# Row sums of squares by ScalarE from a second layout of x, and layer B's first operands made beside layer A's out-projection

## The chip, the cores and the metric

The kernel runs on one core of a Trainium2 chip. TensorE (PE) does the matrix products, VectorE (DVE) and ScalarE (ACT) prepare their operands and take up their results, GpSimd (POOL) does elementwise sums, and SyncE (SP) issues nearly all DMAs from one in-order queue. The metric is the device time of one execution in microseconds (us); lower is better.

## The reference

Two layers on x of 2048 tokens by 1024 features, all in fp32:

```python
for i in range(2):
    h = rmsnorm(x, norm_g[i])        # x * 1/sqrt(mean(x*x) + eps) * g, per token
    x = x + (recurrent_mixer if i == 0 else shortconv_mixer)(h, ...)
return rmsnorm(x, final_g)
```

Layer A (the recurrent mixer): an in-projection from 1024 to 2 x 1536 channels, a causal convolution of 4 taps, two gates by products of 12 heads of 128, a linear recurrence over the tokens, a SiLU gate, and an out-projection from 1536 to 1024. Layer B (the short convolution): an in-projection from 1024 to 4 x 1536 channels, a convolution of 3 taps between two elementwise products, a SiLU gate and an out-projection.

What matters here is the norm. Each token has one factor 1/sqrt(mean of its squares), and the products need it along the free axis: features lie on the partitions and tokens along the row, so the kernel wants the factor as a tile of 128 x 512 with the same row in each partition.

## The kernel before, in words

**Tiling.** The tokens are cut in four chunks of 512. A chunk of x is eight tiles of 128 features x 512 tokens (xs). A fp32 product is done as three f16 products: each operand is split into a high half (ACT, a copy to f16, L297 for x and L403 for weights) and a low half (DVE, the difference, L299 and L404), and `mm3` multiplies high by high, high by low and low by high (L483, L486, L487) into one of six accumulators in PSUM. A product for layer A or B therefore waits for one DVE instruction per operand tile, the low half. Before the split DVE norms a tile of x in place (L291), which needs the factor `inv`.

**The factors in layer A.** Chunk 0 adds up squares in SBUF and sums them over partitions on PE. Chunks 1, 2 and 3 use `inv_by_products`: ACT squares each of the eight tiles (L269), PE multiplies each by a matrix of ones in fp32 (L272), which sums over the partitions and leaves the result in every partition, ACT takes the root (L276) and DVE the reciprocal of 128 x 512 (L277). The generator `second()` does this for chunks 2 and 3 and makes their operands, while PE runs the first products of layer A (`in_A`).

**The out-projection of layer A** (`outA.run`, its first product at 624.3 us, its last at 876.6 us) goes over 4 chunks x 8 blocks of 128 output features. It calls back `emitA` for each finished block: DVE adds the product to the residual x (L1332), SP stores it as layer B's input x2 (chunks 2 and 3 also stay in SBUF), ACT squares it (L216), POOL adds the squares up (L217). After a chunk `endA` makes its factor: PE sums over partitions (L223), then ACT and DVE make 1/root. For chunks 0 and 2 the result goes through DRAM by two DMAs that POOL issues (L239, L240); for chunk 1 by small fp32 products with a diagonal matrix (dg, pn; L246, L249).

**Beside it** runs `besideA(c, d)` with n = 8c + d, the number of the block. It loads and squares the first two weight units of layer B for their scales (L1355, L365; `unit_scale` sums on PE, L374), makes the weight operands of the first unit (`unit_weights`; the sums of weight blocks ws are POOL's, L455), and makes layer B's first activation operands (`build_h`: B11, T1, T2, B21, B22, T3, T4, for k = 0 to 3; each is an element sum or a plain block of the normed x of chunks 0 and 1, split into halves). Layer B's first unit (`in_B`, `unit`) multiplies A11 by B11 (tile p), S1 by T1 (r), S2 by T2 (q) and so on; p opens at once behind the last block of A.

**Order.** The program is written out by a tile scheduler that sets the order of each engine ahead of time from priorities (`tc.high_priority`) and from the order in the code; `after(a, b)` pins a behind b, `in_order` keeps SP's loads in the order in which they were written. At run time each engine works through its list and stops at the first instruction whose input or buffer isn't ready.

Of the kernel before, what the change touches and what calls it, by code (L numbers as in the profile page):

```python
# [31 lines left out]
FIXED = NPC + P + 1 + 2 * (4 + 2 * KB) + 13 * NH + 2 * NH + 19 + 32 + 3 * CH + 66  # L32
# [14 lines left out]
def trunk(ctx, tc, xT, prm, wa, ga, oa, wb, ob, out):  # L47
# [100 lines left out]
    zjunk = keep(CH)  # L148
    tapt, gut = ([keep(n) for i in range(2)] for n in (8, 1))
# [165 lines left out]
    def build_h(l, x, inv, ks, ops, ready=()):  # L315
# [8 lines left out]

        t1, t2 = {}, {}
        for k in ks:
            norm(k, 0)
            add(ops, "B11", k, x[k, 0])
# [13 lines left out]
        for k in ks:  # L342
            norm(k + 4, 0)
            add(ops, "B21", k, x[k + 4, 0])
# [925 lines left out]
    x1 = {(d, c): load("A", d, 2 + c, xt("xs")) for c in range(2) for d in range(KB)}  # L1270
# [3 lines left out]
    def second():  # L1274
        h = build_blocks(0, x1, inv1, hA[1])
        for c in range(2):
            for _ in range(4 - 2 * c):
                yield
            inv_by_products(
                [x1[d, c] for d in range(KB)], inv1[c], split0[1][0], blocks_last[0]  # L1280
            )
            yield
            for _ in range(2):
                next(h)
                yield
# [43 lines left out]
    early, sws, xB = [], [], {}  # L1329
# [17 lines left out]

    def besideA(c, d):
        n = KB * c + d
        if n in (12, 15):  # L1350
            raw = []
            u = (n - 12) // 3
            for q in range(4):
                raw.append(op32("ws"))
                in_order(sp.dma_start(raw[q], wb[u][:, q * CH : (q + 1) * CH]))  # L1355
            sws.append(unit_scale(1, *unit_squares(raw)))
        if n < 17:
            return
        if n == 17:
            early.append(unit_weights(1, wb[0], w0, sws[0]))  # L1360
        if n in (17, 24):
            ks = (0, 1) if n == 17 else (2, 3)
            x = {
                (k, cc): load("B", k, cc, sgt("xs"))
                for a in ks
                for k in (a, a + 4)
                for cc in range(2)
            }
            early.insert(0, build_h(1, x, inv[0], ks, hB[0]))
        advance(early)  # L1370
        if n >= 24:
            advance(early)
# [13 lines left out]
    for d in range(KB):  # L1386
        normed(1, x[d, 0], d, inv[1][0])
# [203 lines left out]
```

## Time and profile before

| | before |
|---|---|
| median of 3 runs | 2043.05 us (2041.72 to 2635.88) |
| profiled execution | 2048.05 us, span 2046.3 us, mean granted PE clock 0.993 |
| PE busy | 2006.7 us, 98% |
| DVE busy | 1178.1 us, 58% |
| ACT busy | 964.2 us, 47% |
| POOL busy | 522.9 us, 26% |
| DMA | 167.22 MB, mean 82 GB/s |

The span is that of the profiled execution, from the first to the last instruction; its own time is 1.75 us longer. Engine shares are means over very different stretches, so the page's table by slices and the windows of the trace are read beside them. In a row of the trace "x5" stands for five like instructions in a run, and square brackets give the engine's idle time before the row and what ended it. Line numbers are those of the kernel before; in the changed kernel the same lines stand a few further down.

### The profile page before, as it was taken

Reading aid. Unit: us, or ns where it says so; the run is one execution under the profiler, and the core shown is the slowest. Engines: PE = TensorE matmul, PEld = TensorE weight load, DVE = VectorE, ACT = ScalarE, POOL = GpSimd, SP = SyncE. Lnnn points to the kernel's source line nnn. Section 1 sums busy time; section 2 is a strip of 40 time slices with the busy share of each in tenths; the row PEclk is TensorE's granted clock in tenths of the full one; section 3 lists DMA queues with packets and bytes.
Section 4 is the critical chain, followed back from the end, with each engine's and each line's share of the span. In section 5 each row is a group of like instructions: output and inputs, shape, how many; then the busy total and the mean of one; then the engine's idle time right before and its main releaser. Section 6 shows DMA issues by size and latency. Waiting matters only on the chain.

```text
span 2046.3 us, 25185 instructions
## 1 busy us (share of the span) xinstructions
PE 2006.7 (98%) x9366; PEld 949.1 (46%) x9366; DVE 1178.1 (58%) x2042; ACT 964.2 (47%) x1756; POOL 522.9 (26%) x437
## 2 busy tenths in 40 slices
PE   8999999999999999978999999999999999999997
PEld 3444444444444444433444444444444444444476
DVE  8977665657474427579636446437437346463323
ACT  7778786868583423234433342343433423443211
POOL 0011010101010213354543433424424424213220
PEclk9999999999999999989999999999999999999998
DMA  7011213042105523411021021121121110574111
GB/s 239 0 52 57 89 51 104 30 166 91 59 22 180 181 75 146 108 67 42 31 93 33 30 86 38 37 93 42 47 78 37 57 42 6 184 279 145 62 40 49
DMA packets 92859, 167.22 MB, mean 82 GB/s; under 512 B 10368, under 2 KB 14080, under 8 KB 92736
## 3 DMA queue, kind: packets, MB, share of 16 engines
q1 hardware_dynamic: 92176, 164.29, 24.0%
q0 software_dynamic: 560, 1.32, 0.3%
q8 instruction: 73, 1.20, 0.3%
q14 instruction: 50, 0.41, 0.1%
HBM read 123.62 MB, written 41.95 MB: 81 GB/s over the span
## 4 chain that ended last, share of the span: by engine, by line
PE 90%; DVE 5%; issue 2%; DMA 2%; ACT 1%; POOL 1%; SPq 0%; DVEq 0%; POOLq 0%; ACTq 0%
PE acc L486 14%; PE acc L487 14%; PE acc L483 14%; PE q L487 6%; PE q L486 6%; PE q L483 6%; PE pg L839 4%; PE p L487 4%; PE p L486 4%; PE p L483 4%; PE r L483 4%; PE r L486 4%; PE r L487 4%; DVE op L299 2%; DVE xs L291 1%
## 5 line engine op out<-in xcount | busy, mean ns | idle before, releaser
L486 PEld LDWEIGHTS <-wc 128*128 128x128 f16 x2096 | 205.4, 98 | 265.3 <-issue 32.2
L483 PEld LDWEIGHTS <-wc 128*128 128x128 f16 x2096 | 208.2, 99 | 253.1 <-issue 17.6
L487 PEld LDWEIGHTS <-wc 128*128 128x128 f16 x2096 | 205.6, 98 | 257.9 <-issue 16.4
L483 PE MATMUL acc<-zs,wf 128*128 128x512 f16 (+1 forms) x864 | 307.8, 356 | 0.0
L486 PE MATMUL acc<-zs,wf 128*128 128x512 f16 (+1 forms) x864 | 307.7, 356 | 0.0
L487 PE MATMUL acc<-zs,wf 128*128 128x512 f16 (+1 forms) x864 | 306.9, 356 | 0.0
L486 PE MATMUL acc<-op,wc 128*128 128x512 f16 x752 | 284.8, 379 | 2.9 <-DVE op L299 2.9
L487 PE MATMUL acc<-op,wc 128*128 128x512 f16 x752 | 285.0, 379 | 0.0
L483 PE MATMUL acc<-op,wc 128*128 128x512 f16 x752 | 283.8, 379 | 0.0
L483 PE MATMUL q<-op,wc 128*128 128x512 f16 x576 | 218.2, 380 | 7.1 <-DVE pb L522 4.2
L487 PE MATMUL q<-op,wc 128*128 128x512 f16 x576 | 219.5, 381 | 0.0
L486 PE MATMUL q<-op,wc 128*128 128x512 f16 x576 | 219.1, 380 | 0.0
L864 POOL TENSOR_TENSOR u<-fixed,u 128x512 f32<-128x512 f32 x48 | 51.3, 1089 | 564.5 <-ACT fixed L861 564.5
L404 DVE SCALAR_TENSOR_TENSOR wc<-ws,fixed,wc 128x512 f16<-128x512 f32 x100 | 98.3, 985 | 98.2 <-ACT wc L403 97.7
L486 PE MATMUL p<-op,wc 128*128 128x512 f16 x384 | 146.3, 381 | 0.0
L483 PE MATMUL p<-op,wc 128*128 128x512 f16 x384 | 146.3, 381 | 0.0
L487 PE MATMUL p<-op,wc 128*128 128x512 f16 x384 | 146.2, 381 | 0.0
L487 PE MATMUL r<-op,wc 128*128 128x512 f16 x384 | 145.7, 379 | 0.0
L486 PE MATMUL r<-op,wc 128*128 128x512 f16 x384 | 145.5, 379 | 0.0
L483 PE MATMUL r<-op,wc 128*128 128x512 f16 x384 | 145.5, 379 | 0.0
L217 POOL TENSOR_TENSOR sa<-sa,sq 128x512 f32<-128x512 f32 x49 | 66.8, 1363 | 241.8 <-ACT sq L216 224.8
L931 POOL TENSOR_TENSOR pb<-pb,cg 128x512 f32<-128x512 f32 x48 | 65.8, 1371 | 230.0 <-ACT pb L548 149.1
(178 smaller groups left out, 3078.2 us busy)
## 6 DMA issues: line engine op xcount, KB each, us to landing
wr<-in_wb SPq DMA_DIRECT2D x100, 256.0 KB, 3.3
xs<-in_xT SPq DMA_DIRECT2D x48, 256.0 KB, 5.4
zA<-sg SPq DMA_DIRECT2D x48, 256.0 KB, 2.0
zr<-zA SPq DMA_DIRECT2D x48, 256.0 KB, 5.3
zB<-ed SPq DMA_DIRECT2D x48, 256.0 KB, 2.0
zr<-zB SPq DMA_DIRECT2D x48, 256.0 KB, 5.3
wr<-in_wa SPq DMA_DIRECT2D x44, 256.0 KB, 4.0
xr<-x SPq DMA_DIRECT2D x32, 256.0 KB, 5.3
```

Of the source, the lines that this page charges most:

```text
L217: squared[0] = eng.tensor_tensor(out=acc, in0=acc, in1=sq, op=ALU.add)
L291: return v.scalar_tensor_tensor(out=x, in0=x, scalar=gs[l][:, kk : kk + 1], in1=inv, op0=ALU.mult, op1=ALU.mult)
L299: return hi, v.tensor_tensor(out=t[:, 1, :], in0=src, in1=t[:, 0, :], op=ALU.subtract)
L404: v.scalar_tensor_tensor(out=t[:, 1, :], in0=src, scalar=sw[:, 2:3], in1=t[:, 0, :], op0=ALU.mult, op1=ALU.subtract,)
L483: ins = nc.tensor.matmul(acc, wh, xh, start=start, stop=False, **kw)
L486: nc.tensor.matmul(acc, wh, xl, start=False, stop=False, **kw)
L487: return nc.tensor.matmul(acc, wl, xh, start=False, stop=stop, **kw)
L839: ins = nc.tensor.matmul(pg, gw[m][:, oo], u, start=True, stop=True)
L864: g.tensor_tensor(out=u, in0=w, in1=u, op=ALU.mult)
L931: g.tensor_tensor(out=t, in0=t, in1=cg[m, half, c], op=ALU.mult)
```

## The change

**Chunks 2 and 3 of layer A.** `inv_by_products` is no longer called for them. Instead x is also given to the kernel in its token-row layout (`in_xn`, 2048 x 1024; no arithmetic is done outside), four tiles of 128 tokens x 1024 features are loaded per chunk (4 x 512 KB), and ACT squares each in place and sums along the row in the same instruction (`accum_out`). That leaves the sums of 512 tokens as 128 x 4. `inv_from` then makes the factor: a root and a reciprocal of 128 x 4, four diagonal matrices by DVE (dg), four small fp32 products by ones (pn) and a copy of 128 x 512 from PSUM.

**Beside A's out-projection.** The loads and squares for the scales of layer B's first two weight units move from n = 12 and 15 to n = 1 and 3, the first unit's weight operands from n = 17 to n = 5. B11 and B21 (chunk 0) of all k are made at n = 10 to 13, and `build_h`, still started at n = 17 and 24, skips them. The tiles of layer B's x have their own names but lie in the twelve buffers of "xs". From n = 24 on, one step instead of two is taken per block. The norm of chunk 2 moves from behind the out-projection to n = 28 to 31.

```diff
--- before
+++ after
...
@@ -146,6 +146,7 @@
     zsc = [keep(3) for c in range(4)]
     gts = [buf(cst, f"gts{m}", f"gts{m}", 1) for m in range(2)]
     zjunk = keep(CH)
+    rows = [keep(4) for c in range(2)]
     tapt, gut = ([keep(n) for i in range(2)] for n in (8, 1))
     tailt = [[[keep(3) for c in range(4)] for m in range(2)] for i in range(2)]
     ws2 = keep(2 * CH).rearrange("p (m c) -> p m c", m=2)
@@ -322,10 +323,14 @@
                 if evac_last[0] is not None:
                     after(ins, evac_last[0])
 
+        def block(name, k, kk, c):
+            if (name, k) not in ops:
+                norm(kk, c)
+                add(ops, name, k, x[kk, c])
+
         t1, t2 = {}, {}
         for k in ks:
-            norm(k, 0)
-            add(ops, "B11", k, x[k, 0])
+            block("B11", k, k, 0)
         yield
         for k in ks:
             norm(k, 1)
@@ -340,8 +345,7 @@
             add(ops, "T2", k, t2[k])
         yield
         for k in ks:
-            norm(k + 4, 0)
-            add(ops, "B21", k, x[k + 4, 0])
+            block("B21", k, k + 4, 0)
         yield
         for k in ks:
             add(ops, "B22", k, x[k + 4, 1])
@@ -1267,18 +1271,29 @@
     w0["behind"] = split0[1][0]
     run(prep0)
     head = first_done(accs, inv0[0], split0[1][1])
-    x1 = {(d, c): load("A", d, 2 + c, xt("xs")) for c in range(2) for d in range(KB)}
+    x1, xrows = {}, [[], []]
+    for c in range(2):
+        for i in range(4):
+            t = wk.tile([P, D], F32, tag="xn", name="xn", bufs=4)
+            xrows[c].append(t)
+            r0 = (2 + c) * CH + i * P
+            sp.dma_start(t, xn[r0 : r0 + P, :])
+        for d in range(KB):
+            x1[d, c] = load("A", d, 2 + c, xt("xs"))
     run(blocks0)
     constants()
 
     def second():
+
         h = build_blocks(0, x1, inv1, hA[1])
         for c in range(2):
+            for i, t in enumerate(xrows[c]):
+                ins = s.activation(t, t, AF.Square, accum_out=rows[c][:, i : i + 1])
+                after(ins, split0[1][0])
             for _ in range(4 - 2 * c):
                 yield
-            inv_by_products(
-                [x1[d, c] for d in range(KB)], inv1[c], split0[1][0], blocks_last[0]
-            )
+            with tc.high_priority(PR):
+                inv_from(rows[c], inv1[c], None, v.tensor_copy, blocks_last[0])
             yield
             for _ in range(2):
                 next(h)
@@ -1326,7 +1341,7 @@
     run(preA)
 
     hB, inv, sums, w0 = [{}, {}], {}, {}, {}
-    early, sws, xB = [], [], {}
+    early, sws, xB, xh = [], [], {}, {}
 
     def emitA(c, d, xr, acc, undo, ts):
         evac_last[0] = v.scalar_tensor_tensor(
@@ -1345,31 +1360,38 @@
             return
         inv_of(sums[c], inv[c // 2][c % 2], g if c in (0, 2) else None)
 
+    def load_h(kk, c):
+        xh[kk, c] = load("B", kk, c, buf(wk, "xh", "xs", 12))
+
     def besideA(c, d):
+
+
         n = KB * c + d
-        if n in (12, 15):
+        if n in (1, 3):
             raw = []
-            u = (n - 12) // 3
+            u = (n - 1) // 2
             for q in range(4):
                 raw.append(op32("ws"))
                 in_order(sp.dma_start(raw[q], wb[u][:, q * CH : (q + 1) * CH]))
             sws.append(unit_scale(1, *unit_squares(raw)))
-        if n < 17:
-            return
-        if n == 17:
+        if n == 5:
             early.append(unit_weights(1, wb[0], w0, sws[0]))
+        if n >= 10 and n < 14:
+            k = n - 10
+            for kk, name in ((k, "B11"), (k + 4, "B21")):
+                load_h(kk, 0)
+                normed(1, xh[kk, 0], kk, inv[0][0])
+                add(hB[0], name, k, xh[kk, 0])
         if n in (17, 24):
             ks = (0, 1) if n == 17 else (2, 3)
-            x = {
-                (k, cc): load("B", k, cc, sgt("xs"))
-                for a in ks
-                for k in (a, a + 4)
-                for cc in range(2)
-            }
-            early.insert(0, build_h(1, x, inv[0], ks, hB[0]))
+            for k in ks:
+                load_h(k, 1)
+                load_h(k + 4, 1)
+            early.append(build_h(1, xh, inv[0], ks, hB[0]))
+        if n >= 28:
+            for kk in range(2 * n - 56, 2 * n - 54):
+                normed(1, xB[kk, 2], kk, inv[1][0])
         advance(early)
-        if n >= 24:
-            advance(early)
 
     def kept_x(d, c):
         def tile():
@@ -1383,8 +1405,6 @@
     while early:
         run(early.pop(0))
     w0 = w0, ahead(1, wb[1], sws[1])
-    for d in range(KB):
-        normed(1, x[d, 0], d, inv[1][0])
     acc3 = sums[3]
 
     def second_half():
...
```

**How the order of instructions moves.** First, layer A's start, around the factor of chunk 2. On PE, before (ss is the sum of squares, acc the accumulators of A's first units):

```order
L487 LDWEIGHTS wc
L487 MATMUL acc<-op,wc 128x512
L486 LDWEIGHTS wc
L486 MATMUL acc<-op,wc 128x512
L487 LDWEIGHTS wc
L487 MATMUL acc<-op,wc 128x512
L272 MATMUL ss<-sq,fixed 128x512 x8
L483 LDWEIGHTS wc
L483 MATMUL acc<-op,wc 128x512
L486 LDWEIGHTS wc
```

and in the changed kernel (pn is the spread-out factor):

```order
L491 LDWEIGHTS wc
L491 MATMUL acc<-op,wc 128x512
L490 LDWEIGHTS wc
L490 MATMUL acc<-op,wc 128x512
L491 LDWEIGHTS wc
L491 MATMUL acc<-op,wc 128x512
L250 MATMUL pn<-dg,fixed 128x128 x4
L487 LDWEIGHTS wc
L487 MATMUL acc<-op,wc 128x512
```

Eight fp32 products of 512 columns are replaced by four of 128, which wait for DVE's dg instead of ACT's squares. On ACT at the same place, before (sq are the squares of chunk 2, u starts the convolution of the first unit, junk are squares of weights):

```order
L365 ACTIVATE junk,fixed<-w_150 128x512
L365 ACTIVATE junk,fixed<-w_151 128x512
L269 ACTIVATE sq<-xs 128x512
L365 ACTIVATE junk,fixed<-w_152 128x512
L365 ACTIVATE junk,fixed<-w_153 128x512
L269 ACTIVATE sq<-xs 128x512 x5
L800 ACTIVATE u<-xb,fixed 128x512
L269 ACTIVATE sq<-xs 128x512
L800 ACTIVATE u<-xb,fixed 128x512
L269 ACTIVATE sq<-xs 128x512
L297 ACTIVATE op<-xs 128x512
```

and now:

```order
L369 ACTIVATE junk,fixed<-w_150 128x512
L369 ACTIVATE junk,fixed<-w_151 128x512
L1291 ACTIVATE xn,fixed<-xn 128x1024 x4
L369 ACTIVATE junk,fixed<-w_152 128x512
L369 ACTIVATE junk,fixed<-w_153 128x512
L804 ACTIVATE u<-xb,fixed 128x512 x2
L236 ACTIVATE r<-fixed 128x4
L298 ACTIVATE op<-xs 128x512 x2
L1291 ACTIVATE xn,fixed<-xn 128x1024
L896 ACT_TABLE_LOAD
L896 ACTIVATE sg<-acc,fixed 128x512 x2
```

The four long squares of chunk 2 stand ahead of both u; those of chunk 3 follow further back.

Second, DVE in the middle of the out-projection of A, only in the changed kernel (xr is a block's residual, zs the operands of the next chunk of the out-projection, xs and op layer B's x of chunk 0):

```order
L1347 SCALAR_TENSOR_TENSOR xr<-acc,fixed,xr 128x512
L1064 TENSOR_SCALAR fixed<-fixed 128x1
L1072 SCALAR_TENSOR_TENSOR zs<-zr,fixed,zs 128x512 x4
L292 SCALAR_TENSOR_TENSOR xs<-xs,fixed,inv 128x512 x2
L1072 SCALAR_TENSOR_TENSOR zs<-zr,fixed,zs 128x512
L292 SCALAR_TENSOR_TENSOR xs<-xs,fixed,inv 128x512 x4
L1072 SCALAR_TENSOR_TENSOR zs<-zr,fixed,zs 128x512
L300 TENSOR_TENSOR op<-xs,op 128x512
L292 SCALAR_TENSOR_TENSOR xs<-xs,fixed,inv 128x512
L300 TENSOR_TENSOR op<-xs,op 128x512
L292 SCALAR_TENSOR_TENSOR xs<-xs,fixed,inv 128x512
L300 TENSOR_TENSOR op<-xs,op 128x512
```

The eight norms need the factor of chunk 0; half of the zs stand behind the first of them, and so does a block's xr.

Third, the end of A's out-projection. On DVE, before (xs<-acc takes up a block, wc is the low half of a weight, op that of an x operand):

```order
L404 SCALAR_TENSOR_TENSOR wc<-ws,fixed,wc 128x512
L404 SCALAR_TENSOR_TENSOR wc<-wr,fixed,wc 128x512
L404 SCALAR_TENSOR_TENSOR wc<-ws,fixed,wc 128x512
L299 TENSOR_TENSOR op<-t_6719,op 128x512
L299 TENSOR_TENSOR op<-t_6725,op 128x512
L299 TENSOR_TENSOR op<-xs,op 128x512 x4
L404 SCALAR_TENSOR_TENSOR wc<-ws,fixed,wc 128x512
L404 SCALAR_TENSOR_TENSOR wc<-wr,fixed,wc 128x512
L1332 SCALAR_TENSOR_TENSOR xs<-acc,fixed,xs 128x512
L404 SCALAR_TENSOR_TENSOR wc<-wr,fixed,wc 128x512
L1332 SCALAR_TENSOR_TENSOR xs<-acc,fixed,xs 128x512 x3
```

and now:

```order
L1347 SCALAR_TENSOR_TENSOR xs<-acc,fixed,xs 128x512
L344 TENSOR_TENSOR t_6812<-xs,t_6756 128x512
L300 TENSOR_TENSOR op<-t_6806,op 128x512
L300 TENSOR_TENSOR op<-t_6812,op 128x512
L300 TENSOR_TENSOR op<-xs,op 128x512 x4
L300 TENSOR_TENSOR op<-t_6806,op 128x512
L1347 SCALAR_TENSOR_TENSOR xs<-acc,fixed,xs 128x512
L300 TENSOR_TENSOR op<-t_6812,op 128x512
L300 TENSOR_TENSOR op<-xs,op 128x512 x4
L1347 SCALAR_TENSOR_TENSOR xs<-acc,fixed,xs 128x512 x4
```

The weights' low halves among the last blocks are gone, made earlier. On POOL at the same place (sa adds up squares, ws sums weight blocks), before:

```order
L217 TENSOR_TENSOR sa<-sa,sq 128x512
L455 TENSOR_TENSOR ws<-wr 128x512
L217 TENSOR_TENSOR sa<-sa,sq 128x512
L455 TENSOR_TENSOR ws<-wr 128x512
L455 TENSOR_TENSOR ws<-ws,wr 128x512
L217 TENSOR_TENSOR sa<-sa,sq 128x512 x3
L455 TENSOR_TENSOR ws<-wr,ws 128x512
```

and now:

```order
L459 TENSOR_TENSOR ws<-ws,wr 128x512
L218 TENSOR_TENSOR sa<-sa,sq 128x512
L358 TENSOR_TENSOR t_6806<-xs,t_6806 128x512
L358 TENSOR_TENSOR t_6812<-xs,t_6812 128x512
L218 TENSOR_TENSOR sa<-sa,sq 128x512 x5
L459 TENSOR_TENSOR ws<-wr,ws 128x512
L459 TENSOR_TENSOR ws<-wr 128x512
```

The sums of squares of the last five blocks now stand together, with no ws between them.

## Rows read from the trace of the kernel before

**Rows 1.** PE's waits over the span: engine, line, waited for: total us, times, longest.

```profile
PE ss L223 <- POOL sa L217: 7.5, 1, 7.5
...
PE q L483 <- DVE pb L522: 4.2, 1, 4.2
...
PE acc L486 <- DVE op L299: 2.9, 3, 1.7
```

**Rows 2.** Timeline of PE, 20 to 80 us: start us, us, engine, line, op.

```profile
23.75 1.05 PE L249 MATMUL pn<-dg,fixed 128*128 128x128 f32 x8
...
54.46 7.03 PE L272 MATMUL ss<-sq,fixed 128*128 128x512 f32 x16
61.33 0.38 PE L483 MATMUL acc<-op,wc 128*128 128x512 f16 x1
...
71.26 7.03 PE L272 MATMUL ss<-sq,fixed 128*128 128x512 f32 x16
```

**Rows 3.** Timeline of DVE at 63 us and at 894 us.

```profile
63.59 3.35 DVE L277 RECIPROCAL inv<-inv 128x512 f32<-128x512 f32 x1 [2.84 <-ACT inv L276]
...
894.77 0.88 DVE L246 TENSOR_SCALAR dg<-fixed,r 128x128 f32<-128x128 f32 x4
```

**Rows 4.** Timeline of ACT at 39 us, and line L861's long activation (ns min/median/max).

```profile
39.27 2.70 ACT L269 ACTIVATE sq<-xs 128x512 f32<-128x512 f32 x5
...
L861 ACT ACTIVATE fixed<-fixed x24: 1056/1057/1059, 102.4 to 613.4; 128x1024 f32<-128x1024 f32 x24
```

**Rows 5.** Windows: us, then each engine's busy us (instructions), PEclk, DMA share, GB/s.

```profile
23.00:29.00 6.00, 6.00 (x22) 3.13 (x21) 4.09 (x7) 4.66 (x9) 0.00 (x0) 1.00 0.01 2
...
50.00:75.00 25.00, 23.28 (x84) 10.51 (x83) 21.66 (x32) 15.90 (x26) 0.00 (x0) 1.00 0.01 2
```

**Rows 6.** Timeline of PE, 876 to 893 us.

```profile
876.85 0.38 PE L483 MATMUL p<-op,wc 128*128 128x512 f16 x1
877.06 0.38 PE L486 MATMUL p<-op,wc 128*128 128x512 f16 x1
...
882.96 0.38 PE L483 MATMUL q<-op,wc 128*128 128x512 f16 x1 [0.77 <-DVE xs L1332]
...
892.36 1.87 PE L223 MATMUL ss<-fixed,sa 128*128 128x1 f32 x8 [7.52 <-POOL sa L217]
```

**Rows 7.** Windows by stage, the columns of rows 5.

```profile
700.00:725.00 25.00, 25.00 (x117) 11.34 (x116) 10.41 (x17) 13.91 (x29) 5.31 (x5) 1.00 0.53 140
725.00:750.00 25.00, 25.00 (x120) 11.71 (x119) 5.07 (x12) 3.11 (x5) 3.85 (x3) 1.00 0.09 32
...
850.00:875.00 25.00, 25.00 (x118) 11.36 (x116) 25.00 (x24) 13.79 (x25) 18.21 (x12) 1.00 0.13 46
...
895.00:900.00 5.00, 5.00 (x15) 1.83 (x14) 2.06 (x6) 0.14 (x1) 0.00 (x0) 0.56 0.00 0
```

**Rows 8.** Timeline of DVE, 840 to 886 us.

```profile
840.94 6.05 DVE L291 SCALAR_TENSOR_TENSOR xs<-xs,fixed,inv 128x512 f32<-128x512 f32 x9 [3.30 <-DMA inv<-rd]
...
858.18 1.75 DVE L299 TENSOR_TENSOR op<-xs,op 128x512 f16<-128x512 f32 x1
...
872.01 1.28 DVE L299 TENSOR_TENSOR op<-xs,op 128x512 f16<-128x512 f32 x2
...
883.49 2.05 DVE L1332 SCALAR_TENSOR_TENSOR xs<-acc,fixed,xs 128x512 f32<-128x512 f32 x3
```

**Rows 9.** Timeline of POOL, 887 to 893 us.

```profile
887.57 4.73 POOL L217 TENSOR_TENSOR sa<-sa,sq 128x512 f32<-128x512 f32 x3
```

**Rows 10.** Timeline of SP's queue, 645 to 690 us.

```profile
652.07 6.72 SPq L1048 DMA_DIRECT2D zr<-zA  x12
...
679.02 1.64 SPq L1335 DMA_DIRECT2D x<-xr  x2
```

**Rows 11.** Tile ws, 640 to 800 us, its loads' landing; POOL's timeline at 716 us.

```profile
DMA to landing us min/median/max: 5.4/7.7/13.1
...
715.89 0.56 POOL L240 DMA_DIRECT2D inv<-rd  x1 [11.80 <-DMA ws<-in_wb]
```

More of the change, by code (lines that the diff above doesn't have):

```diff
@@ L31 @@
 NPC = 284
-FIXED = NPC + P + 1 + 2 * (4 + 2 * KB) + 13 * NH + 2 * NH + 19 + 32 + 3 * CH + 66
+FIXED = NPC + P + 1 + 2 * (4 + 2 * KB) + 13 * NH + 2 * NH + 19 + 32 + 3 * CH + 66 + 8
 KH = NH // 2
@@ L46, in trunk @@
 @with_exitstack
-def trunk(ctx, tc, xT, prm, wa, ga, oa, wb, ob, out):
+def trunk(ctx, tc, xT, xn, prm, wa, ga, oa, wb, ob, out):
     nc = tc.nc
@@ L1571 @@
         "in_xT": i["x"][0].T,
+        "in_xn": i["x"][0],
         "in_prm": prm,
```

## The prediction

> **What bounds the kernel now.** I read the page's shares first (PE busy 98%, the next engine 58%), then PE's waits, then the timelines where PE stands still or does work that the change removes, and last the engines on which those places wait. PE's whole idle time is some 40 us, and the page's chain of waits gives PE 90% of the span, so a gain can only come from PE work that goes away or from one of the few waits. The largest wait, 7.5 us for POOL's sum of squares, is one that the change bears on; the 4.2 us wait for DVE further on isn't, and the 2.9 us for DVE's low halves lies where the change works [rows 1]. So there are two places: layer A's first 100 us, and the passage from A's out-projection to layer B around 880 us. In between PE is fed without a stop, so what is won at the first place is carried to the second, if nothing new stops PE on the way.
>
> **First place: the squares of chunks 2 and 3.** Removed from PE are two groups of eight fp32 products; each holds PE for 61.33 - 54.46 = 6.87 us, the second like the first [rows 2]: -13.7 us. Added are two groups of four small products, 1.05 us each as the same helper shows for another chunk [rows 2]: +2.1 us. Net -11.6 us of PE work.
>
> Whether PE gets all of it hangs on DVE, which is nearly full here (21.66 of 25 us [rows 5]). Two reciprocals of 3.35 us go, one with 2.84 us of waiting before it [rows 3]. In their place each chunk has four dg at 0.88 us for the four [rows 3] and a copy, which I put at 0.7 us since other 128 x 512 operations on DVE take 0.64 to 0.74 (an estimate from a low half [rows 8]): 1.6 us against 3.35. DVE gains 3.5 us or more, and the waits. But the added dg of both chunks now stand on DVE's queue ahead of low halves of chunk 1, where PE already follows DVE (the 2.9 us [rows 1]). ACT loses sixteen squares at 0.54 us, 8.6 us [rows 4], and gains eight long ones at 1.06 us [rows 4], about 9 us with the read of the sum: even in amount, but four of them, 4.4 us, now stand in a block ahead of the convolution's u, and DVE waits behind that for about 1.6 us (my walk through the new order with these durations: u becomes ready at 43.4 instead of 41.9). While PE follows DVE, to about 62 us, it can't run ahead; by the same walk the product that starts at 61.33 before starts at about the same time after it, with the first 6.87 us spent on waiting for low halves in part. Take 2.6 us for that: gain 9. Ends: 11.6 if DVE never becomes the limit, 6 if both chunks' dg, copies and ACT's block all land on PE's path (11.6 - 2 x 1.6 - 1.6 - 0.8).
>
> The eight loads of the second layout, 4.2 MB, cost nothing in the sum: the first four are issued near 17 us and have the stretch to 29 us, in which the DMA share is 0.01 [rows 5], before ACT wants them at 37.5; the other four wait for the first squares and are wanted from about 46 us. The f32 loads of x behind them on SP's queue come about 8 us later than before but are wanted only from 62 us on.
>
> **The middle: work moved under the out-projection.** All of it is work that was there before, and PE is at work at every moment of this stretch, so it costs nothing as long as nobody's wait reaches PE. The nearest to doing so are three. (1) PE's two sums for the weights' scales wait for ACT's squares, which wait for loads. SP issued its loads of zr from 652.07 and, but for three more loads, was idle before 679.02 [rows 10]; the four loads of the first unit stand behind ten of these, at about 657. Landing took 5.4 to 13.1 us, median 7.7 [rows 11], the four squares some 2.8 us, the same again for the second unit, whose buffers come free with the first squares: 657 + 2 x (7.7 + 2.8) = 678, at the worst 689, against PE reaching the second sum at about 686 (counted back in the new order from 876.85 at 0.2155 us a product, between the 0.21 of [rows 6] and 0.22). I take 0, with 8 as the far end. (2) DVE's norms of chunk 0 wait for the factor that went through DRAM: POOL issued its last DMA at 715.89, held for 11.80 us by weight loads that are now out of its way [rows 11]. It would land by about 727. Behind the norms stand operands of the out-projection's next chunk, which PE wants when that chunk begins, two chunks of 8 x 36 products at 0.2155 us before 876.85, so at 752: 0. (3) The moved norms and low halves, sixteen on DVE at 0.64 to 1.75 us [rows 8], at most 28 us, go where DVE is busy 10.41 and 5.07 of 25 us [rows 7]: 0.
>
> **Second place: the end of the out-projection.** DVE runs without a gap from 840.94 to 885.5 us, through 51 instructions, and the last three blocks of A are taken up at 883.49 only [rows 8], although PE had finished the last block before 876.85 [rows 6]. POOL then sums three squares in 4.73 us [rows 9] with sums of weights queued between, and PE, which comes to its sum of squares at 892.36 - 7.52 = 884.84, waits until 892.36 [rows 6]. After that the clock is granted at 0.56 of full from 895 to 900, which is the lower level of 1.2 GHz for most of it [rows 7].
>
> In the new order the same stretch of DVE's list has 36 instructions; eight low halves of x, and seven of weights, are gone from it. At the stretch's own mean, 44.6 / 51 = 0.87 us, they take 32 us: DVE is at the last block at about 873, ahead of PE. The last block is then taken up at 877.6, squared at 878.3 and added at about 880, while PE reaches its sum at 884.84 - 0.77 = 884.1: 4 us to spare. So 0.77 + 7.52 = 8.3 us of waiting go, and with them the low clock: from 892.36 to about 900, 7.6 us, PE ran at that share and so lost 0.44 x 7.6 = 3.4 us. Together -12. Everything behind starts that much earlier in the same order, and the 4.2 us wait [rows 1] stays.
>
> Here a DVE instruction's time is the unknown. A low half took 1.75 us at 858.18 and 0.64 at 872.01 [rows 8], long ones where POOL was at work. At 0.64 the 36 end at 864, at 1.75 for all at 904, which is later than before; the mean of the stretch is nearest, since POOL is busy 18.21 of 25 us there before [rows 7] and has the same or fewer sums after. The Trainium skill's page SBUF — State Buffer (two separate sides) says why: DVE instructions with two SBUF inputs and GpSimd share one port pair, an exclusive lock for a whole instruction. By that rule the time hangs on whether POOL's sums still lie beside DVE's; the trace agrees with it in the two durations.
>
> **Sum.** -9 - 12 = -21 us on 2048.05: 2027. This execution is 5.0 us above the median of 2043.05, so I forecast 2022 for the median.
>
> **Rivals.**
> - *DVE still ends last at A's end* (15%). POOL's sums lie beside DVE's remaining instructions: 36 x 0.64 and POOL's some 20 us of blocking end at about 884. Then the wait stays at some 6 us with the low clock, stage two gives 2, the sum is -11: 2032. For it: the 1.75 us; against it: 15 instructions fewer in any case.
> - *The first place gives nothing* (9%). The second layout lands late or ACT's block of squares delays DVE more than walked, so that PE waits where it squared: gain 0 to 3, the sum -13: 2030. Against it: DMA stands at 0.01 to 29 us.
> - *It ends slower* (9%): an in-order wait in the middle. If the loads for the second scale are held until after 686 (behind weight loads and stores on SP's queue), PE stands at its sum for landing and squares, 13.1 + 2.8, and twice if the first is late too: 32 us, and some us of low clock behind each; less 21 gained, about 2055. It decides when these loads are issued some 20 us later than I reckon, near 677. SP's idle time speaks against that.
> - *More comes free* (7%): no loss at the first place (11.6), and the wait of 4.2 us and its like behind it shrink as DVE comes out of A early: -11.6 - 12 - 6 = -30: 2013.
> - The forecast itself: 60%, between 2016 and 2028.
>
> **Range and chances.** From 2011 to 2040: it takes in all but the slower case and the far ends of the first two rivals, with the bounds above (6 to 11.6, 2 to 18, 0 to 8). Two per cent, about what a measurement of this kernel can tell from no change, is 41 us: faster than 2002 would need every wait of the passage gone and more (2%); slower than 2084 needs the slower rival at more than twice its price (3%); within 2% is left with 95%.
>
> **What would show it.** PE's timeline has no L272 group at 54 and 71 us, two groups of pn, and the products of chunk 2 about 9 us earlier by 100 us; PE's waits lack the 7.5 us for POOL, with the granted clock at its higher level from 885 to 905; no new wait on the weights' squares between 650 and 880 us. I am wrong if PE's waits show a new line of several us in the first 100 us or in the out-projection, or if the last blocks are still taken up by DVE long after PE has finished them.

## The result, and the profile after

| | before | changed |
|---|---|---|
| median | 2042.38 us (4 runs, 2041.51 to 2635.88) | 2023.74 us (4 runs, 2022.28 to 2026.06) |
| ratio to before | 1 | 0.9911, 95% interval 0.9892 to 0.9931 |
| profiled execution | 2048.05 us, span 2046.3 | 2022.28 us, span 2020.5 |
| PE busy | 2006.7 us | 1988.8 us |
| mean granted PE clock | 0.993 | 0.997 |

The changed kernel takes 18.6 us less, 0.9%: within 2%, faster beyond the interval, and 1.7 us above the forecast of 2022. Without the slow run of 2635.88 us the median of before is 2041.72, and the gain 18.0 us. The two profiled spans differ by more, 25.8 us; the second trace of before (last experiment) shows why.

PE's waits after; columns as in [rows 1]:

```profile
PE pt L122 <- ACT fixed L118: 4.5, 1, 4.5
...
PE q L487 <- DVE pb L526: 4.3, 1, 4.3
PE acc L490 <- DVE op L300: 2.8, 3, 1.7
...
PE acc L487 <- ACT op L298: 1.3, 1, 1.3
PE pg L843 <- ACT tg L847: 1.1, 1, 1.1
```

The 7.5 us for POOL's sum is gone. The waits for pb (4.3) and for low halves (2.8) stayed. Two small waits for ACT are new, 1.3 and 1.1 us. From 600 to 850 us PE was busy 250.00 of 250 us in both kernels, so the middle gave and cost nothing to PE.

**First place.** PE after, 20 to 70 us (start us, us, engine, line, op, and in brackets the idle time before):

```profile
22.00 1.05 PE L250 MATMUL pn<-dg,fixed 128*128 128x128 f32 x8
...
26.33 7.03 PE L273 MATMUL ss<-sq,fixed 128*128 128x512 f32 x16
...
49.12 0.59 PE L487 MATMUL acc<-op,wc 128*128 128x512 f16 x2 [1.27 <-ACT op L298]
...
51.45 0.59 PE L490 MATMUL acc<-op,wc 128*128 128x512 f16 x1 [1.74 <-DVE op L300]
55.25 1.05 PE L250 MATMUL pn<-dg,fixed 128*128 128x128 f32 x8
...
68.44 1.05 PE L250 MATMUL pn<-dg,fixed 128*128 128x128 f32 x8
```

Only chunk 1's group of squares is left, at 26.33; the two groups of [rows 2] at 54 and 71 us are pn groups of 1.05 us. The wait of 1.27 us is for a high half (48.45) that stands right behind one of ACT's long squares of chunk 3 (47.41). The four of chunk 2 stand in a block from 35.78 on. On ACT:

```profile
35.78 1.04 ACT L1291 ACTIVATE xn<-xn 128x1024 f32<-128x1024 f32 x1
36.73 0.19 ACT L1291 ACTIVATION_READ_ACCUMULATOR xn<-xn 128x1 f32 x1
36.82 1.04 ACT L1291 ACTIVATE xn<-xn 128x1024 f32<-128x1024 f32 x1
...
47.41 1.06 ACT L1291 ACTIVATE xn<-xn 128x1024 f32<-128x1024 f32 x1
...
48.45 0.63 ACT L298 ACTIVATE op<-xs 128x512 f16<-128x512 f32 x1
```

From start to start they take 1.04 us with the read of the sum: eight are 8.3 us where "about 9" was reckoned.

**Second place.** The end of A's out-projection after, first on DVE (the take-ups of the last blocks):

```profile
857.49 1.40 DVE L1347 SCALAR_TENSOR_TENSOR xs<-acc,fixed,xs 128x512 f32<-128x512 f32 x2
860.13 0.75 DVE L1347 SCALAR_TENSOR_TENSOR xs<-acc,fixed,xs 128x512 f32<-128x512 f32 x1 [1.25 <-PE acc L491]
867.90 0.75 DVE L1347 SCALAR_TENSOR_TENSOR xs<-acc,fixed,xs 128x512 f32<-128x512 f32 x1 [7.02 <-PE acc L491]
```

Then POOL's last sum of squares, and PE at its first p behind the last block and at the sum over partitions:

```profile
869.46 1.27 POOL L218 TENSOR_TENSOR sa<-sa,sq 128x512 f32<-128x512 f32 x1 [6.46 <-ACT sq L217]
```

```profile
867.70 0.38 PE L487 MATMUL p<-op,wc 128*128 128x512 f16 x1
...
874.61 0.95 PE L224 MATMUL ss<-fixed,sa 128*128 128x1 f32 x8
```

The direction of waiting has turned round. In [rows 8] DVE took up the last three blocks at 883.49, long after PE had finished them; now DVE stands idle for 7.02 us until PE has finished the last one. POOL's sum ends at 869.46 + 1.27 = 870.7 and PE comes to its sum of squares at 874.61 without waiting (no bracket), against 7.52 us in [rows 6]. The windows, columns as in [rows 5]:

```profile
875.00:900.00 25.00, 22.88 (x113) 11.12 (x114) 20.98 (x22) 8.91 (x18) 16.19 (x11) 1.00 0.00 0
895.00:900.00 5.00, 3.71 (x18) 1.71 (x18) 5.00 (x5) 0.00 (x0) 4.92 (x5) 1.00 0.00 0
```

The granted clock stays at its higher level, 2.4 GHz, where [rows 7] had 0.56 from 895 to 900. What is missing from 5 us in the 3.71 is the end of a 2.1 us wait for DVE's cg, which before has as well.

**The middle.** SP's loads of ws, and DVE at the moved norms:

```profile
648.78 2.33 SPq L1375 DMA_DIRECT2D ws<-in_wb  x4
...
655.13 5.84 SPq L1375 DMA_DIRECT2D ws<-in_wb  x4
```

```profile
694.32 0.75 DVE L1347 SCALAR_TENSOR_TENSOR xr<-acc,fixed,xr 128x512 f32<-128x512 f32 x1
...
711.00 1.41 DVE L292 SCALAR_TENSOR_TENSOR xs<-xs,fixed,inv 128x512 f32<-128x512 f32 x2 [13.16 <-DMA inv<-rd]
...
719.43 0.74 DVE L1347 SCALAR_TENSOR_TENSOR xr<-acc,fixed,xr 128x512 f32<-128x512 f32 x1
```

DVE stood 13.16 us for the factor from DRAM. One block's take-up (694.32) had gone ahead of the norms, the next (719.43) waited behind them in DVE's list. PE didn't stop for it.

### The profile page after: what moved, and what is told of

It reads as the page before. It is cut to its first block, busy times and chain, and to the rows that moved or that the text cites. A ratio compares the mean times of both kernels' runs of the same rounds, so it can differ in the third digit from the quotient of the medians.

```text
span 2020.5 us, 25191 instructions
## 1 busy us (share of the span) xinstructions
PE 1988.8 (98%) x9350; PEld 942.3 (47%) x9350; DVE 1171.5 (58%) x2052; ACT 960.6 (48%) x1754; POOL 528.8 (26%) x437
## 4 chain that ended last, share of the span: by engine, by line
PE 90%; DVE 5%; issue 2%; ACT 2%; DMA 1%; POOL 0%; SPq 0%; DVEq 0%; ACTq 0%; POOLq 0%
PE acc L490 14%; PE acc L491 14%; PE acc L487 14%; PE q L487 6%; PE q L491 6%; PE q L490 6%; PE r L487 4%; PE p L490 4%; PE p L491 4%; PE p L487 4%; PE r L491 4%; PE r L490 4%; PE pg L843 3%; DVE op L300 1%; DVE u L806 1%
## 5 line engine op out<-in xcount | busy, mean ns | idle before, releaser
L487 PEld LDWEIGHTS <-wc 128*128 128x128 f16 x2096 | 207.9, 99 | 253.7 <-issue 18.9
L490 PEld LDWEIGHTS <-wf 128*128 128x128 f16 x864 | 84.8, 98 | 81.1
```

The costliest lines, as they stand in the source:

```text
L487: ins = nc.tensor.matmul(acc, wh, xh, start=start, stop=False, **kw)
L490: nc.tensor.matmul(acc, wh, xl, start=False, stop=False, **kw)
```

## The experiments

The executions are compared by five stretches between landmarks on PE, which every trace has: from the span's start to the first pn products (those of chunk 0's factor in layer A); from there to the small sum pt in the convolution's part of A (116.07 before, 105.33 after); from the first pn to the first pt of 128 x 24 (450.85, 441.70), which holds the second stretch; from that to the same in layer B (1567.63, 1544.92), which holds the middle and the passage from A to B; and the rest. The first, third, fourth and fifth add up to the span.

| us in one profiled execution | to first pn | first pn to pt | first pn to 128x24 in A | A to B | rest | median |
|---|---|---|---|---|---|---|
| before | 23.75 | 92.32 | 427.10 | 1116.78 | 478.67 | 2042.38 |
| before again | 22.12 | 92.33 | 427.33 | 1113.99 | 475.96 | |
| changed | 22.00 | 83.33 | 419.70 | 1103.22 | 475.58 | 2023.74 |
| rows only | 24.11 | 83.07 | 418.79 | 1115.07 | 475.73 | 2035.48 |
| beside only | 23.80 | 92.33 | 427.06 | 1103.78 | 475.46 | 2031.38 |
| no early blocks | 23.95 | 83.38 | 420.23 | 1103.14 | 475.48 | 2024.89 |
| no early weights | 23.65 | 83.08 | 420.25 | 1117.54 | 475.96 | 2039.05 |
| the same, factor by products | 24.38 | 83.34 | 420.67 | 1105.55 | 475.30 | 2027.47 |
| squares unpinned | 22.49 | 88.15 | 427.79 | 1104.27 | 475.25 | 2033.72 |
| chunk 2 early too | 24.16 | 83.40 | 420.48 | 1108.30 | 475.76 | 2029.66 |
| that, factors by products | 22.24 | 83.40 | 420.49 | 1105.75 | 475.82 | 2027.22 |
| factors by products | 22.22 | 83.38 | 419.97 | 1104.89 | 476.02 | 2028.03 |

The first column takes one of two values, about 22.2 or 24, in kernels with the same head, before among them (23.75 and 22.12): it is a matter of the execution, and of the granted clock in it. The windows from 20 to 25 us, of before and of before again:

```profile
20.00:25.00 5.00, 5.00 (x16) 2.65 (x15) 2.92 (x6) 5.00 (x10) 0.00 (x0) 0.79 0.54 194
20.00:25.00 5.00, 5.00 (x19) 2.77 (x18) 4.57 (x8) 5.00 (x10) 0.00 (x0) 1.00 0.43 152
```

In the five traces with the short head the clock stands at 1.00 here, in the seven with the long one at 0.66 to 0.82. With the stretch from 15 to 20 us the missing share comes to 1.7 us in each of the seven (before: 0.13 x 5 + 0.21 x 5, an estimate), which is the difference. Why the clock falls in some executions isn't shown; PE's wait just ahead is 0.9 to 3.1 us in the seven and 1.3 to 2.0 in the five. The second to fourth columns are where the kernels differ.

### One part of the change at a time

The second layout alone: `besideA` is that of before, `second()` is the changed one. And the reverse: `besideA` is changed, `second()` is that of before.

```diff
# beside only, in second()
-            for i, t in enumerate(xrows[c]):
-                ins = s.activation(t, t, AF.Square, accum_out=rows[c][:, i : i + 1])
...
-                inv_from(rows[c], inv1[c], None, v.tensor_copy, blocks_last[0])
+            inv_by_products(
+                [x1[d, c] for d in range(KB)], inv1[c], split0[1][0], blocks_last[0]
+            )
```

> The first part of the change alone: row sums from the second layout for chunks 2 and 3; layer B's operands are made as before. My theory (two separate gains that add): the blocks of A come 9 us earlier, the wait of 7.5 us for POOL's sums and the low clock at A's end stay, so about 9 us faster than before, near 2033 us, ratio 0.9955. Rival (the low-clock passage at A's end depends on where in time it falls, or the second place gave more than 12 of the gain): 4 us faster or less. Rival (the first place gave nearly all): 16 or more faster.

> The second part alone: layer B's first weight scales, first unit and chunk 0's operands made early beside A's out-projection; chunks 2 and 3 of layer A squared by ACT and summed by PE as before. My theory: the L272 groups stay at 54 and 71 us, A's blocks end at about 876.9 as before, PE's wait of 7.5 us for POOL's sum is gone and the clock stays at its upper level there, so about 12 us faster than before, near 2030. Rival (the parts need each other, for instance because ACT or DVE is fuller without the first): gain under 6.

Measured: rows only 2035.48, ratio 0.9967 [0.9954, 0.998], -6.7 us; beside only 2031.38, ratio 0.9948 [0.9934, 0.9963], -10.8 us. Together -17.5, against -18.6 for both: the parts add up. Each moves its own column of the table and leaves the other as it was. PE at A's end with the rows only, and its window:

```profile
883.32 1.86 PE L224 MATMUL ss<-fixed,sa 128*128 128x1 f32 x8 [7.34 <-POOL sa L218]
```

```profile
875.00:900.00 25.00, 17.66 (x77) 8.91 (x76) 13.37 (x20) 10.87 (x22) 15.18 (x12) 0.80 0.24 81
```

The wait and the low clock are like those of before. With the work beside A only, PE's sum starts at 884.33 without a wait, DVE idles 7.02 us before the last take-up, and the clock is 1.00 from 875 to 900. So the passage's gain comes from the moved work alone.

### Which of the moved work counts

First without the blocks B11 and B21 at n = 10 to 13 (all of `build_h` at n = 17 and 24, two steps a block from 24 on); then with these blocks, but the weights' scales at n = 12 and 15 and their operands at n = 17, behind `build_h`, with two steps a block from 24 on, as before.

```diff
# no early blocks
-        if n >= 10 and n < 14:
-            k = n - 10
-            for kk, name in ((k, "B11"), (k + 4, "B21")):
...
# no early weights
-        if n in (1, 3):
+        if n in (12, 15):
...
-        if n == 5:
+        if n == 17:
             early.append(unit_weights(1, wb[0], w0, sws[0]))
```

> The changed kernel without one piece: B11 and B21 of chunk 0 are made in build_h again (from block 17 on); the weight scales and the first unit stay early. DVE has about 45 instructions from the first norm of chunk 2 to the last block of A in place of 36. Theory that DVE's count at A's end decides (0.87 us each): DVE reaches the last block about 1 to 2 us after PE has finished it, which the 3.9 us to spare at PE's sum cover, so 0 to 2 us slower than the changed kernel (2024 to 2026). Rival that the early blocks are what took the wait away: the wait of about 7 us and the low clock are back, 10 us or more slower than the changed kernel.

> The changed kernel without the other piece: the weight scales are loaded at blocks 12 and 15 and the first unit's operands made from block 17 on, as before; B11 and B21 stay early. DVE has about 46 instructions in that stretch, and POOL has sums of weights ahead of the last sums of squares. Theory that DVE's count decides: about 1 to 3 us late, covered, 0 to 2 us slower than the changed kernel. Theory that POOL's queue decides (weight sums in front of the last four sums of squares): PE's wait for POOL is back with 2 to 5 us, and with it part of the low clock: 2 to 8 us slower (2026 to 2032).

Measured: without early blocks 2024.89, ratio 0.9917 [0.9902, 0.9932], the changed kernel's time within the intervals. DVE takes up three of the last blocks together at 868.06, later than in the changed kernel, but PE still comes to its sum at 877.09 without a wait. Beside the early weights, the early blocks are worth nothing that these runs can tell.

Without early weights 2039.05, ratio 0.999 [0.9981, 1.0]: 15 us lost against the changed kernel, 14.3 of them in the stretch from A to B. Neither theory had put them where they are. At A's end little is lost, though DVE takes up the last four blocks only at 882.36: PE waits 1.24 us for POOL, and the clock is 1.00 from 875 to 900.

```profile
889.55 1.05 PE L224 MATMUL ss<-fixed,sa 128*128 128x1 f32 x8 [1.24 <-POOL sa L218]
```

PE's largest wait is elsewhere:

```profile
PE acc L487 <- DVE xr L1347: 8.3, 1, 8.3
```

What led to it, on POOL, on DVE and on PE, and the windows around it:

```profile
703.17 0.56 POOL L241 DMA_DIRECT2D inv<-rd  x1 [11.30 <-DMA ws<-in_wb]
```

```profile
687.45 0.75 DVE L1347 SCALAR_TENSOR_TENSOR xr<-acc,fixed,xr 128x512 f32<-128x512 f32 x1 [5.73 <-PE acc L491]
...
708.85 2.74 DVE L292 SCALAR_TENSOR_TENSOR xs<-xs,fixed,inv 128x512 f32<-128x512 f32 x4 [14.02 <-DMA inv<-rd]
711.51 0.74 DVE L1347 SCALAR_TENSOR_TENSOR xr<-acc,fixed,xr 128x512 f32<-128x512 f32 x1
```

```profile
712.30 0.58 PE L487 MATMUL acc<-zs,wf 128*128 128x512 f16 x1 [8.32 <-DVE xr L1347]
```

```profile
705.00:710.00 5.00, 0.00 (x0) 0.00 (x0) 1.15 (x2) 0.37 (x1) 0.00 (x0) 0.79 0.84 278
710.00:715.00 5.00, 2.70 (x7) 0.99 (x7) 5.00 (x9) 4.78 (x10) 1.94 (x1) 0.50 0.14 54
715.00:720.00 5.00, 5.00 (x18) 1.91 (x16) 4.91 (x7) 3.02 (x9) 0.78 (x1) 0.69 0.00 0
```

This is an in-order wait in the middle, the kind of the slower rival. SP issues the loads of ws at 690.59 instead of 648.78; POOL's second DMA for the factor starts at 703.17, put down to these loads; DVE stands 14.02 us at a norm; behind that norm in DVE's list stands the take-up of a block whose accumulator PE needs next; PE stands 8.32 us, and then runs at the lower level of 1.2 GHz (0.50, 0.69) for some us. This wait, the low clock (2.70 x 0.50 + 5.00 x 0.31 = 2.9 us, an estimate) and the 1.24 us at A's end make 12.5 of the 14.3 us. The changed kernel has nearly the same wait on DVE, 13.16 us, and PE doesn't notice. The loads make little of the difference: from POOL's first DMA to DVE's first norm it is 17.9 us here (690.95 to 708.85) and 17.2 in the changed kernel (693.79 to 711.00). DVE's list makes it: ahead of the norms the changed kernel has the take-ups of ten blocks (the last at 694.32), this one of nine (the last at 687.45), and the tenth is the one at 711.51 that PE stands for.

To test whether the wait hangs on the factor's way through DRAM, the same kernel was run with chunk 0's factor spread by four small products, as chunk 1's is:

```diff
-        inv_of(sums[c], inv[c // 2][c % 2], g if c in (0, 2) else None)
+        inv_of(sums[c], inv[c // 2][c % 2], g if c == 2 else None)
```

> As e4 (early blocks, weights late), but the factor of chunk 0 for layer B is spread by small products on PE, as chunk 1's is, and not through DRAM. Theory that e4's new wait (8.3 us of PE, behind DVE that sat 14.0 us for the factor's DMA, plus the low clock after it) comes from the factor's way through DRAM: both are gone, one group of small products (about 1 us) is added: 2039 - 8.3 - 3.5 + 1, near 2028. Rival (DVE's order or its count at A's end is the cause): it stays at 2035 or above.

Measured: 2027.47, ratio 0.9925 [0.9908, 0.9941], as the theory said; no wait of PE from 600 to 850 us. SP issues the loads as late as before this edit (691.33), but DVE's norms start at 696.95 in place of 708.85. The stretch from A to B falls from 1117.54 to 1105.55. What is left against the changed kernel includes a wait at A's end:

```profile
880.28 1.05 PE L224 MATMUL ss<-fixed,sa 128*128 128x1 f32 x8 [1.35 <-POOL sa L218]
```

So late weights, with the added products, cost the passage some 2 us (1105.55 against 1103.22, this wait among them), and 12 us more where the factor of chunk 0 goes through DRAM.

### Where ACT's long squares stand

The four long squares of chunk 2 are no longer pinned behind the splitting of chunk 0, so the scheduler may put them anywhere.

```diff
                 ins = s.activation(t, t, AF.Square, accum_out=rows[c][:, i : i + 1])
-                after(ins, split0[1][0])
+                if c:
+                    after(ins, split0[1][0])
```

> The changed kernel, where ACT's four long squares of chunk 2 are no longer held behind the second operand of the first chunks, so they move ahead of eight high halves of chunk 1. Theory that the block of squares ahead of the convolution cost the first place 1 to 2 us: 2021 to 2023. Rival (what the first place loses it loses where ACT is full between 150 and 225 us): no change, 2023 to 2025. Rival (they now delay chunk 1's operands, which PE waits for): 1 to 5 us slower.

Measured: 2033.72, ratio 0.9956 [0.9941, 0.9971], 10 us slower than the changed kernel, by the second rival's mechanism at twice its price (1 to 5 us). Now the four long squares of chunk 2 start at 25.47 and from 28.07 on, between high halves, and the four of chunk 3, still pinned, stand in a block from 42.80 to 46.97, ahead of high halves. PE waits for these:

```profile
45.92 1.04 ACT L1291 ACTIVATE xn<-xn 128x1024 f32<-128x1024 f32 x1
...
47.58 0.62 ACT L298 ACTIVATE op<-xs 128x512 f16<-128x512 f32 x1
```

```profile
48.24 0.98 PE L487 MATMUL acc<-op,wc 128*128 128x512 f16 x2 [4.04 <-ACT op L298]
...
53.37 1.01 PE L487 MATMUL acc<-op,wc 128*128 128x512 f16 x2 [2.19 <-ACT op L298]
```

Of the first place's 9 us 4.2 are left at pt, and none at 128x24 (waits of 3.2 us for ACT's tg and 1.6 us for DVE's u come behind). The second layout pays only while its squares are out of the way of high halves.

### More of the same

The blocks B11 and B21 of chunk 2, whose norms are made at n = 28 to 31, are split there too; then the same with all three factors by products; then the changed kernel with all factors by products.

```diff
# chunk 2 early too
-            for kk in range(2 * n - 56, 2 * n - 54):
+            k = n - 28
+            for kk, name in ((k, "B11"), (k + 4, "B21")):
                 normed(1, xB[kk, 2], kk, inv[1][0])
+                add(hB[1], name, k, xB[kk, 2])
# factors by products
-        inv_of(sums[c], inv[c // 2][c % 2], g if c in (0, 2) else None)
+        inv_of(sums[c], inv[c // 2][c % 2], None)
```

> The changed kernel, and B11 and B21 of chunk 2 made as well beside the last four blocks of A, where DVE has 7 us free. Six low halves (0.6 us each) go ahead of A's end. Theory that PE's waits after A's end (2.1, 2.6 and 4.3 us in the changed kernel) are DVE's backlog: they shrink by about 4 us together, 2020. Rival (they hang on ACT or on weight loads): no change, 2023 to 2025. Rival (DVE now ends late at A's end, more than the 3.9 us to spare): slower by the excess and part of the low clock.

> As e11, and the factors of chunks 0 and 2 for layer B spread by small products in place of the way through DRAM. Adds two groups of small products to PE (about 1.8 us) and lets DVE start on both chunks some 10 us earlier. Theory that DVE's time at A's end is what binds after it: 2 to 4 us faster than the changed kernel, near 2020. Rival (nothing waits for these factors any more): 1 to 2 us slower than e11.

> The changed kernel with the factors of chunks 0 and 2 of layer B spread by four small products instead of two DMAs through DRAM. Costs on PE: two more groups of products, 1.1 to 1.9 us each, so +2 to +4. Theory (the chain through DRAM, which held DVE 13.2 us in the changed kernel without stopping PE, is off PE's path): nothing is won for that, 2024 to 2028. Rival (that hold costs PE something further on, through operands made later): 2018 to 2022, and the waits for low halves around 890 to 920 us shrink.

Measured: chunk 2 early 2029.66, ratio 0.9939 [0.9924, 0.9953]; with factors by products 2027.22, 0.9924 [0.9909, 0.9939]; the changed kernel with factors by products 2028.03, 0.9928 [0.9916, 0.994]. None beats the changed kernel. The first is 6 us slower in none of the ways expected: PE comes to its sum at A's end without a wait, but there are two waits for pb where there was one.

```profile
925.31 0.59 PE L487 MATMUL q<-op,wc 128*128 128x512 f16 x1 [4.22 <-DVE pb L526]
945.36 0.58 PE L487 MATMUL q<-op,wc 128*128 128x512 f16 x1 [3.84 <-DVE pb L526]
```

The second is most of the 5.1 us by which the stretch from A to B is longer. Why DVE is later at the second pb wasn't followed further. The second kernel fits neither of its expectations: it is 3.5 us slower than the changed kernel where 2 to 4 faster was expected, and 2.4 faster than the first where the rival had 1 to 2 slower. The last comes out at the upper end of its theory (2024 to 2028): the 13 us hold of DVE in the middle cost PE nothing, so removing it didn't pay. Its stretch from A to B is 1.7 us longer, with two groups of products more and waits for pb of 6.2 us in place of 4.3; what the products cost by themselves isn't separated. Its median is 4.3 us up, with intervals that overlap.

### The kernel before, a second trace

> The kernel before, unchanged, for a second trace. If the last 400 us of the first trace (404.3 us from the first small products of layer B's end to the last instruction, 401.1 to 401.6 in the variants) are a matter of that one execution, they take 401 to 402 here and the wait for the last DVE take-ups is some tenths of a us; if they belong to the kernel before, 404 again.

Measured: 2041.15, one run; span 2039.4, 6.9 us below the first trace of the same kernel. Its waits:

```profile
PE ss L223 <- POOL sa L217: 6.5, 1, 6.5
...
PE q L483 <- DVE pb L522: 2.6, 1, 2.6
...
PE ss L1463 <- DVE sa L1432: 0.3, 1, 0.3
```

The rest takes 475.96, as in all the others: the first trace's 478.67 (a wait of 1.9 us at L1463 and a clock of 0.84 from 1995 to 2005) was that execution's. The head is 1.6 us shorter, with the clock at 1.00, and the stretch from A to B 2.8 us, with smaller waits for POOL and for pb. Against this trace the changed kernel's span is 18.9 us shorter (0.1 + 7.6 + 10.8 + 0.4), near the difference of the medians, 18.6.

## Why the prediction held

The forecast was -21 us, the medians show -18.6, inside the forecast's own range of 2016 to 2028. The two places and what changes in them are as forecast. By its steps:

- **First place, -9.** At pt, 105 us, it is -9.0, and -8.9 to -9.3 in all eight traces that have the second layout with its squares pinned. The 13.7 removed and the 2.1 added hold as counted. The 2.6 taken back for waits on low halves is right in size and not in kind, which is luck: those waits didn't grow (2.83 us, against 2.93 before). New are 1.27 us for a high half behind ACT's long square, with which PE's waits grew by 1.2 us (0.55 + 0.54 + 1.27 + 1.74 = 4.10 in the trace), and a clock of 0.66 from 50 to 55 us, where before has 1.00; over 3.54 us of PE's work it makes another 1.2 (an estimate), and the working had no term for it. DVE's wait behind ACT's block of squares, walked as 1.6 us, is 1.12 us. But the term was mis-sized behind that point: at 128x24, 442 us, 7.4 to 7.6 are left in the changed kernel and 6.4 to 8.5 in the eight traces. The 1.6 us go between 140 and 250 us, where PE was busy 110.00 of 110 us before and 108.62 after; the waits are for ACT's tg (1.1) and DVE's sg (0.2). I had taken it that what is won is carried to the second place since PE doesn't stop in between; running ahead, it met ACT, which is busy 22.37 of 25 us from 150 to 175.
- **The middle, 0.** Right. Of the three candidates the first had its loads issued at 648.78, as reckoned (657, less the 9 us won before); the last square began at 671.90, and PE came to its second sum at 677.20 without a wait. The second held DVE 13.16 us without stopping PE, though the weight loads that were out of its way had been little of it: POOL's hold between the two DMAs fell only from 11.80 to 9.53 us.
- **Second place, -12.** Against the two traces of before the stretch from A to B gives -13.6 and -10.8. DVE's stretch, for which 36 instructions of 0.87 us were reckoned, took 33 instructions from 829.70 to 858.89, 0.88 us each, and then the last two take-ups, for which DVE waits. (Before, the trace has 50 instructions there, 0.89 us each, where 51 were counted.) The 4 us to spare at PE's sum are 3.9 (870.7 to 874.61). The 4.2 us wait for pb stayed, as said. A wait of 1.3 us for cg at the weights' sum (L374) went as well, which the sum didn't have.
- **The base.** I set the sum against one execution's span and took its 5 us above the median off as a constant. That was right for the median, but a constant is not what it is: of the 6.9 us between the two traces of before 4.3 lie in the head and the rest, which the change doesn't touch (1.6 + 2.7), -0.2 in the stretch of the first place, and 2.8 in the stretch from A to B, where the wait that the change removes and the one that it leaves are 1.0 and 1.6 us apart. And 2 per cent is more than a measurement of this kernel needs to tell a change from none: the interval here is 0.9892 to 0.9931.
- **The rivals.** That DVE still ends last at A's end is refuted: it idles 7.02 us. That the first place gives nothing is what the unpinned squares show, by the mechanism named (ACT's squares delaying DVE's and PE's operands): the changed order is near that edge, kept off it by one pinned line. The slower rival came true in kind in the kernel without early weights, and not by its trigger or at its place. The loads of ws are late there by the edit (690.59, where 677 was the point), but they are as late (691.33) in the kernel with the factor by products, and there PE doesn't wait. PE stood not at the weights' sum but at a take-up behind DVE's norm, and the price was 15 us, not 33 (2055 against 2022). The working on the norms of chunk 0 had looked behind them for operands, which PE wants at 752 only, and not for the take-up, which frees an accumulator.

What was not foreseen is how the parts of the moved work stand to each other. The prediction took eight low halves of x (by the two traces they are four low halves and four norms) and seven of weights off DVE's last stretch alike. At A's end either part is nearly enough: PE's wait for POOL there, 7.34 us with neither (rows only), is 0 with the early weights alone, and 1.24 us with the early blocks alone (1.35 with the factor by products as well), each time with the clock at 1.00 from 875 to 900. Beside the early weights the blocks give nothing measurable; without them their norms, which wait for the factor through DRAM, cost PE more in the middle than they save at the end: 2039.05 against 2035.48 with the rows only. The kernels with one part also have the norm of chunk 2 at n = 28 to 31; what that does alone, and what the factor by products does in the kernel before, was not run.

In A's last stretch DVE's times also bear on the Trainium skill's page SBUF — State Buffer (two separate sides), which the prediction weighed: in the changed kernel a low half of the same size took 1.75 us at 841.32, while POOL worked from 840.81 to 844.2 without a break, and 0.68 at 853.22, while POOL was idle (from 851.5 to 855.5). The trace agrees with the page's exclusive lock; from 855.55 it is POOL's sum that is long, 3.15 us against 1.27 at 869.46, beside low halves of 0.62 us. Since POOL's work stayed, the stretch's mean of before was the right price.

## What to carry to other kernels

A factor that goes through a queue and back to an in-order engine costs nothing as long as the instruction queued behind the waiting one isn't the one that frees the busy engine's next buffer; whether it is can't be read from the length of the wait (13.16 us cost nothing, 14.02 us cost 8.32 and the clock), only from the list. When work is moved early, undo its pieces one by one, and look where the time is lost and not only how much: here either piece nearly emptied the end of A, and the 15 us of one run were lost in the middle. And read two traces of the kernel before, cut at the same landmarks, before a difference of spans is put down to a change: 6.9 us lay between two executions of the same kernel.

## What the runs showed of the hardware

- An activation of 128 x 1024 with a sum along the row took 1.04 us from start to start, its read of the accumulator (shown as 0.19 us) all but hidden: 35.78, 36.82.
- The head of the program, up to the first pn, takes about 22.2 or about 24 us from one execution to the next, five and seven times in twelve traces, whatever the kernel: the granted clock from 20 to 25 us is 1.00 in the five and 0.66 to 0.82 in the seven.
- A 2 KB factor sent to DRAM and read back to all partitions held POOL 9.53 us between the two DMAs, and DVE got it 6.8 us after the second was issued (704.23 to 711.00), with the DMA engines 0.82 busy from the first DMA to the second and 0.77 from there on.
